# A gated convolution that waits in DRAM as one float32 array and is split into two halves when attention loads it

## The chip, the cores and the metric

The kernel runs on one core of one Trainium2 chip. Its engines are TensorE (PE, with PEld for its weight loads), VectorE (DVE), ScalarE (ACT), GpSimd (POOL) and SyncE (SP), which here issues nearly all transfers between DRAM and the on-chip memory. The metric is the time of one execution on the device in microseconds (us); the number told of a kernel is the median of its runs. The profile is of one further execution, whose own time is given beside its span.

## The reference, cut to what matters

One decoder layer on 1024 tokens of width 1024. A single projection gives ten blocks; four feed a gated convolution, four an attention with 16 heads, two the gates with which the branches are merged.

```python
proj = jnp.einsum("bsd,dc->bsc", h, w_in)
xc, bg, cg, zc, q, k, v, za, g_conv, g_attn = jnp.split(proj, splits, axis=-1)
c = causal_depthwise_conv(cg * xc, conv_w)
y_conv = jnp.einsum("bsc,cd->bsd", jax.nn.silu(zc) * bg * c, w_out_conv)
o = mixture_of_dilations(q, k, v, slopes)
y_attn = jnp.einsum("bsc,cd->bsd", jax.nn.silu(za) * o, w_out_attn)
merged = sigmoid(g_conv) * y_conv + sigmoid(g_attn) * y_attn
return jnp.einsum("bsd,de->bse", merged, w_o)
```

The array of this case is `silu(zc) * bg * c`, here called y: 1024 channels by 1024 tokens, kept in 8 blocks of 128 channels. It is computed early and multiplied by `w_out_conv` much later.

## The kernel before, in words

Every float32 operand of a matmul is written as the sum of a high and a low part in the type float32r. `split(hi, lo, src)` makes them: ScalarE casts (L80), and VectorE, or GpSimd where it is named, subtracts (L81). A product then takes three matmuls (hi x hi, hi x lo, lo x hi).

The program has these stages in time: v (to about 117 us), then the other sections of the projection in pairs (`sec`: q and k, the convolution's four, the gates), attention with its 16 heads (from about 812 us), the attention output, and the last product.

In a section, twelve matmuls make one product, a weight half `a_hi`, `a_lo` is split for it from the tile `raw` or from a sum `s`, and a result leaves the bank through a copy (L352) or an addition `sec_o` (L357). The last section of each channel pair of the convolution ends in `sg` = y (L414). There the kernel before splits `sg` into `qk_hi` (ScalarE) and `qk_lo` (GpSimd) and stores both to `y_dram`, 512 tokens at a time (L415 to L419): 16 pieces. After the convolution the table `tb` for attention's bias is loaded (L426), VectorE computes the bias of the first head (L438), and GpSimd that of each later one (L440, L441).

Attention goes through 64 units, each a head and two query blocks of 128: TensorE makes scores (L462, L463), VectorE adds the bias and finds the extreme `nm` (L467), ScalarE takes exponentials (L472, which also leaves the denominator `den`), TensorE transposes the blocks (L583), ScalarE and VectorE split them into `pp` and `diag` (L80, L81), and TensorE multiplies them by the values `vp` (L594, L595). `scores` runs two units ahead of `values`. Two results of a head are copied out by `otmp` and `ot` (L600, L601). From the second unit of the loop on, every second unit fetches one block c of y into `ghi[:, c]` and `glo[:, c]` (L677 to L680): a tiny copy from `den` into the tile on VectorE comes first, so that the load cannot be issued before attention is that far. Eight blocks of y are fetched in units 2 to 16.

`conv_out(c, h)` is the product of y with `w_out_conv`, 24 matmuls (L98 to L100) for each of 16 pieces; its weights come through `load_w` (L83). The pieces are called from the fifth head on, but their matmuls read one block of y each.

What sets the order: the order of instructions on each engine is not that of the code. The framework sorts them by an estimate of its own of when each could run, and each engine and SP's queue then goes strictly in that order, an instruction that waits holding up all behind it. Tiles named `raw` in the pool `wr` share four buffers of 4 KB per partition, which are given out in the order of the code: first the sections' weights, then in attention the weights and gates (`gc`) of `conv_out`.

Of the kernel before, what the change touches and what calls it, by code (L numbers as in the profile page):

```python
# [11 lines left out]
F32 = mybir.dt.float32  # L12
F32R = mybir.dt.float32r
# [5 lines left out]
P = 128  # L19
S = 1024  # L20
D = 1024
NK = D // P
# [15 lines left out]
def f(ap):  # L38
    return ap.bitcast(F32)
# [3 lines left out]
def layer(ctx, tc, x, norm_g, w_blk, w_v, b_merge, conv_w, w_conv, w_attn, w_o, final_g, tab, sel_in, selb_in, out):  # L43
    nc = tc.nc
# [3 lines left out]
    wr = ctx.enter_context(tc.tile_pool(name="wr", bufs=4, reuse_waits="tile"))  # L48
    small = ctx.enter_context(tc.tile_pool(name="small", bufs=4, reuse_waits="tile"))
    dram = ctx.enter_context(tc.tile_pool(name="dram", bufs=1, space=DRAM))  # L50
# [14 lines left out]
    m_dram = dram.tile([NK, P, S], F32, name="m_dram")  # L65
    r_dram = dram.tile([NP, 32, P], F32, name="r_dram")
    z_dram = dram.tile([NK, P, S], F32, name="z_dram")
    y_dram = dram.tile([2, NK, P, S], F32, name="y_dram")
    g_dram = dram.tile([2, NK, P, S], F32, name="g_dram")
    qk_dram = dram.tile([NP, 4, P, S], F32, name="qk_dram")  # L70

# [7 lines left out]
    def split(hi, lo, src, eng=None):  # L79
        nc.scalar.copy(hi, src)  # L80
        (eng or nc.vector).tensor_sub(lo, src, f(hi))  # L81
# [241 lines left out]
    pc = pc_cm.__enter__()  # L323
# [70 lines left out]
    for c in range(0, NK, 2):  # L394
        xc = pc.tile([P, 2, S], F32, name="xc", bufs=1)
        uu = pc.tile([P, 2, 2 + S], F32, name="uu", bufs=1)
        nc.gpsimd.memset(uu[:, :, 0:2], 0.0)
        for i, t, v in sec(c, c + 1):
            nc.scalar.copy(xc[:, i, t], v)
        for i, t, v in sec(16 + c, 17 + c):  # L400
            nc.vector.tensor_mul(uu[:, i, 2 + t.start:2 + t.stop], v, xc[:, i, t])
        cv = xc
        for i in range(2):
            w3 = cw[:, c + i]
            nc.scalar.mul(cv[:, i], uu[:, i, 2:2 + S], w3[:, 2:3])
            for j in (1, 0):
                nc.vector.scalar_tensor_tensor(cv[:, i], uu[:, i, j:j + S], w3[:, j:j + 1], cv[:, i], op0=OP.mult, op1=OP.add)
        for i, t, v in sec(8 + c, 9 + c):
            nc.vector.tensor_mul(cv[:, i, t], v, cv[:, i, t])
        for i, t, v in sec(24 + c, 25 + c):  # L410
            sg = out_tile()
            nc.scalar.activation(sg, v, AF.Sigmoid)
            nc.vector.tensor_mul(sg, v, sg)
            nc.vector.tensor_mul(sg, sg, cv[:, i, t])  # L414
            hi = pc.tile([P, 512], F32R, name="qk_hi", bufs=1)  # L415
            lo = pc.tile([P, 512], F32R, name="qk_lo", bufs=1)
            split(hi, lo, sg, nc.gpsimd)
            nc.sync.dma_start(y_dram[0, c + i, :, t], f(hi))
            nc.sync.dma_start(y_dram[1, c + i, :, t], f(lo))  # L419
    pc_cm.__exit__(None, None, None)  # L420


# [23 lines left out]
    den, pools = {}, []  # L446
# [95 lines left out]
    with (tc.tile_pool(name="atl", bufs=2, reuse_waits="tile") as atl, tc.tile_pool(name="atm", bufs=2, reuse_waits="tile") as atm,  # L542
# [109 lines left out]
        for i, (hd, bp) in enumerate(units):  # L652
            if i % 4 == 0:
                if hd % 2 == 0:
                    ot[hd // 2] = atl.tile([P, S], F32, name="ot")
                if hd + 1 < NH:
                    load_head(hd + 1)
            if i + LOOK < len(units):
                ready.append(scores(*units[i + LOOK]))
            if i == len(units) - 5:  # L660
                ab = ap0.tile([P, 2, S], F32R, tag="tb", name="a_tb")
                load_act(0, ab[:, 0], ab[:, 1])
                load_act(1, *act_tiles((ap0, "q2", 1), (ap0, "kh", 1)))
                load_act(2, *act_tiles((ap0, "kl", 1), (ap0, "bias", 2)))
            if i == len(units) - 2:
                load_act(3, *act_tiles((ap1, "q2", 1), (ap1, "kh", 1)))
                act7 = act_tiles((ap1, "kl", 1), (ap0, "bias", 2))
                nc.sync.dma_start(f(act7[0]), z_dram[NP - 1])
                sel_b = rrows[1][:32]
                sel_raw = wr.tile([P, S], F32, tag="raw", name="raw")  # L670
                nc.sync.dma_start(sel_raw[:32], selb_in)
                nc.scalar.copy(sel_b, sel_raw[:32])
                gate_last(LAST[1] // 4)
            values(hd, bp, ready.pop(0))
            if i % 2 == 0 and G0 <= i < G0 + 2 * NK:

                c = (i - G0) // 2  # L677
                for g, src in ((ghi, y_dram[0, c]), (glo, y_dram[1, c])):
                    nc.vector.tensor_copy(g[:, c, 0:1], den[hd // 2][:, hd % 2, bp:bp + 1])
                    nc.sync.dma_start(f(g[:, c]), src)  # L680
            if i % 4 == 3:
                if hd in FILLS:
                    conv_out(*divmod(FILLS.index(hd), 2), atn)
                if hd % 2 == 1:
                    divide(hd // 2)
                elif hd:
                    spread(hd // 2 - 1)
                if hd == NH - 1:
                    gate_last(LAST[3] // 4)
                    last_act(*act7)  # L690
                    conv_out(*divmod(FILL, 2), atn)
                    for i in range(FILL + 1, 2 * NK):
                        conv_out(*divmod(i, 2), work, (2, 4))
# [122 lines left out]
```

## Time and profile before

| | |
|---|---|
| median of 3 runs | 1342.55 us (1336.83 to 1343.76) |
| profiled execution | 1339.46 us, its span 1337.7 us |
| TensorE busy | 1290.5 us (96%) |
| VectorE busy | 831.2 us (62%) |
| ScalarE busy | 647.5 us (48%) |
| GpSimd busy | 228.8 us (17%) |
| TensorE's granted clock, mean | 0.988 of full speed |
| moved by DMA | 191.92 MB, of it 58.31 MB written |
| chain of waits that ended last | TensorE 83%, DMA 7%, VectorE 4%, ScalarE 3% |

The shares are means over stages that differ. In the windows view each row is a stretch of time, and for each engine it has the busy time and the number of instructions. "Busy" for a DMA is the mean over the core's 16 DMA engines, and can come out a little above 1. A row of the waits says which instruction stood still, on which engine, and what ended its wait. A row of the timeline has the start, the duration and, in square brackets, the idle time of the engine ahead of it.

### The profile page before, as it was taken

To read this page: it belongs to the slowest core of one execution; us is meant where nothing else is said; L and a number is where in the kernel's file an instruction comes from. 1 tells how busy PE (TensorE), PEld (TensorE's weight loads), DVE (VectorE), ACT (ScalarE), POOL (GpSimd) and SP (SyncE) were. 2 spreads that over 40 slices of the span, in tenths; PEclk is the share of its full clock that TensorE was granted. 3 is DMA by queue.
4 is the path that set the end of the run, shared out by engine and by line. 5 is a ranking of instruction groups with operands and counts; after the bars stand their busy time and mean duration, and the time that the engine had idled before them with its cause. 6 is when DMAs were issued, how large, how long until landed. Compare 5 with 4: busy or idle time off the path is not lost.

```text
span 1337.7 us, 17655 instructions
## 1 busy us (share of the span) xinstructions
PE 1290.5 (96%) x6236; PEld 1069.4 (80%) x6236; DVE 831.2 (62%) x1580; ACT 647.5 (48%) x1271; POOL 228.8 (17%) x170
## 2 busy tenths in 40 slices
PE   9799999999999999999999997889999999999997
PEld 6577888888888888878888886778888988888886
DVE  6965665657677666776554444677677665454325
ACT  7643444444434444344444465777677776222211
POOL 0000000000101000030000002534434455154000
PEclk9999999999999999999999998999999999999999
DMA  7455444422313132163333316986656573555302
GB/s 281 145 173 183 163 173 166 164 81 63 126 48 111 62 102 72 65 211 103 109 120 111 105 63 177 303 228 153 174 145 186 143 241 144 199 189 189 142 32 95
DMA packets 86930, 191.92 MB, mean 143 GB/s; under 512 B 8429, under 2 KB 33261, under 8 KB 86714
## 3 DMA queue, kind: packets, MB, share of 16 engines
q1 hardware_dynamic: 84040, 181.80, 43.1%
q0 software_dynamic: 2800, 9.00, 2.0%
q8 instruction: 49, 0.80, 0.3%
q14 instruction: 39, 0.32, 0.1%
q10 hardware_dynamic: 2, 0.00, 0.0%
HBM read 132.46 MB, written 58.31 MB: 143 GB/s over the span
## 4 chain that ended last, share of the span: by engine, by line
PE 83%; DMA 7%; DVE 4%; ACT 3%; issue 1%; SPq 0%; POOL 0%; DVEq 0%; ACTq 0%
PE bank L346 17%; PE bank L347 17%; PE bank L348 17%; PE bank L98 4%; PE bank L99 4%; PE bank L100 4%; PE bank L583 3%; PE bank L754 2%; PE bank L753 2%; PE bank L752 2%; PE bank L594 2%; PE bank L595 2%; PE bank L462 2%; PE bank L463 2%; DMA v_dram<-v 1%
## 5 line engine op out<-in xcount | busy, mean ns | idle before, releaser
L346 PE MATMUL bank<-t_hi,a_hi 128*128 128x512 f32 x576 | 225.5, 392 | 3.6 <-DVE sec_o L357 3.2
L347 PE MATMUL bank<-t_lo,a_hi 128*128 128x512 f32 x576 | 224.9, 390 | 0.0
L348 PE MATMUL bank<-t_hi,a_lo 128*128 128x512 f32 x576 | 224.9, 390 | 0.0
L80 ACT CAST a_hi<-s 128x512 fp32r<-128x512 f32 x144 | 89.6, 622 | 184.2 <-PE bank L347 167.7
L346 PE MATMUL bank<-b_hi,a_hi 128*128 128x512 f32 x432 | 169.0, 391 | 3.2 <-ACT a_hi L80 3.2
L347 PE MATMUL bank<-b_lo,a_hi 128*128 128x512 f32 x432 | 168.6, 390 | 0.0
L348 PE MATMUL bank<-b_hi,a_lo 128*128 128x512 f32 x432 | 168.4, 390 | 0.0
L81 DVE TENSOR_TENSOR a_lo<-s,a_hi 128x512 fp32r<-128x512 f32 x144 | 103.0, 715 | 93.1 <-ACT a_hi L80 93.1
L80 ACT CAST a_hi<-raw 128x512 fp32r<-128x512 f32 x108 | 67.0, 621 | 145.8 <-PE bank L347 123.3
L346 PEld LDWEIGHTS bank<-t_hi,a_hi 128*128 128x128 f32 x576 | 108.6, 189 | 27.4 <-DVE sec_o L357 3.9
L347 PEld LDWEIGHTS bank<-t_lo,a_hi 128*128 128x128 f32 x576 | 108.7, 189 | 22.5
L348 PEld LDWEIGHTS bank<-t_hi,a_lo 128*128 128x128 f32 x576 | 108.4, 188 | 22.6
L472 ACT ACTIVATE pr<-pr,nm 128x640 f32<-128x640 f32 (+7 forms) x128 | 100.0, 784 | 15.9 <-DVE nm L467 15.4
L346 PEld LDWEIGHTS bank<-b_hi,a_hi 128*128 128x128 f32 x432 | 81.4, 188 | 21.0 <-ACT a_hi L80 4.1
L81 DVE TENSOR_TENSOR a_lo<-raw,a_hi 128x512 fp32r<-128x512 f32 x108 | 74.3, 688 | 36.1 <-ACT a_hi L80 36.1
L348 PEld LDWEIGHTS bank<-b_hi,a_lo 128*128 128x128 f32 x432 | 81.4, 188 | 17.0
L347 PEld LDWEIGHTS bank<-b_lo,a_hi 128*128 128x128 f32 x432 | 81.3, 188 | 16.7
L583 PE MATMUL bank<-ident,pr 128*128 128x128 f32 x576 | 89.7, 276 | 3.3 <-ACT pr L472 2.7
L467 DVE CUSTOM_DVE_ANT_0 pr<-bank,bias 128x512 f32<-128x512 f32 (+3 forms) x128 | 72.0, 569 | 33.6 <-PE bank L463 31.5
L583 PEld LDWEIGHTS bank<-ident,pr 128*128 128x128 f32 x576 | 68.9, 142 | 12.2 <-ACT pr L472 5.3
L81 DVE TENSOR_TENSOR pp<-bank,pp 128x512 fp32r<-128x512 f32 x96 | 64.9, 687 | 19.7 <-ACT pp L80 19.0
L462 PE MATMUL bank<-kh,q 128*128 128x256 f32 (+2 forms) x192 | 73.7, 386 | 1.7 <-ACT sg L492 0.8
(230 smaller groups left out, 2635.3 us busy)
## 6 DMA issues: line engine op xcount, KB each, us to landing
raw<-in_w_blk SPq DMA_DIRECT2D x72, 512.0 KB, 3.6
raw<-in_w_v SPq DMA_DIRECT2D x18, 512.0 KB, 3.8
v_dram<-v SPq DMA_DIRECT2D x16, 512.0 KB, 3.0
qk_dram<-qk_hi SPq DMA_DIRECT2D x32, 256.0 KB, 2.0
qk_dram<-qk_lo SPq DMA_DIRECT2D x32, 256.0 KB, 2.8
q<-qk_dram SPq DMA_DIRECT2D x32, 256.0 KB, 8.1
kh<-qk_dram SPq DMA_DIRECT2D x32, 256.0 KB, 6.4
kl<-qk_dram SPq DMA_DIRECT2D x32, 256.0 KB, 7.5
```

Source lines behind the costliest of these rows:

```text
L80: nc.scalar.copy(hi, src)
L81: (eng or nc.vector).tensor_sub(lo, src, f(hi))
L98: nc.tensor.matmul(pt, whi[:, k, :], mhi[:, t], start=(k == 0), stop=False)
L99: nc.tensor.matmul(pt, whi[:, k, :], mlo[:, t], start=False, stop=False)
L100: nc.tensor.matmul(pt, wlo[:, k, :], mhi[:, t], start=False, stop=(k == NK - 1))
L346: nc.tensor.matmul(pt, hi[:, k], mhi[:, k], start=first and k == 0, stop=False, **more)
L347: nc.tensor.matmul(pt, hi[:, k], mlo[:, k], start=False, stop=False, **more)
L348: nc.tensor.matmul(pt, lo[:, k], mhi[:, k], start=False, stop=k == H - 1, **more)
L462: nc.tensor.matmul(sc[:, :n], qs, kh[hd][:, c0:c0 + n], start=True, stop=False)
L467: nc.vector.tensor_tensor_reduce(pr[:, c0:c0 + m], sc[:, :m], bias[hd][:, off:off + m], 1.0, 3.0e38 if nm is None else nm, OP.add, OP.min, ...
L472: nc.scalar.activation(pr[:, :nk], pr[:, :nk], AF.Exp, bias=nm, scale=-1.0, accum_out=den[p][:, a, b:b + 1])
L583: nc.tensor.transpose(pt[:, j, i * P:(i + 1) * P], rows[b][:, (kb + j) * P:(kb + j + 1) * P], ident)
```

## The change

y goes through DRAM once, in float32. The split before the store is gone, `sg` itself is stored; a block that comes back lands in a tile `raw`, and `split` makes `ghi[:, c]` and `glo[:, c]` of it, on ScalarE and VectorE. The tiny copy from `den` now goes to `raw`.

```diff
-    y_dram = dram.tile([2, NK, P, S], F32, name="y_dram")
+    y_dram = dram.tile([NK, P, S], F32, name="y_dram")
...
             nc.vector.tensor_mul(sg, sg, cv[:, i, t])
-            hi = pc.tile([P, 512], F32R, name="qk_hi", bufs=1)
-            lo = pc.tile([P, 512], F32R, name="qk_lo", bufs=1)
-            split(hi, lo, sg, nc.gpsimd)
-            nc.sync.dma_start(y_dram[0, c + i, :, t], f(hi))
-            nc.sync.dma_start(y_dram[1, c + i, :, t], f(lo))
+            nc.sync.dma_start(y_dram[c + i, :, t], sg)
...
                 c = (i - G0) // 2
-                for g, src in ((ghi, y_dram[0, c]), (glo, y_dram[1, c])):
-                    nc.vector.tensor_copy(g[:, c, 0:1], den[hd // 2][:, hd % 2, bp:bp + 1])
-                    nc.sync.dma_start(f(g[:, c]), src)
+                raw = wr.tile([P, S], F32, tag="raw", name="raw")
+                nc.vector.tensor_copy(raw[:, 0:1], den[hd // 2][:, hd % 2, bp:bp + 1])
+                nc.sync.dma_start(raw, y_dram[c])
+                split(ghi[:, c], glo[:, c], raw)
```

Lines behind the first edit stand four lower in the changed kernel, and behind the second three lower (L472 becomes L468, L438 becomes L434).

On ScalarE, in the third head, the rows of the kernel before, from the exponential of its sixth block to that of its eighth (`rt` belongs to the denominators):

```order
L472 ACTIVATE pr_7208,den<-pr_7208,nm 128x768
L615 CAST rt<-bank 32x128
L80 CAST diag_6700<-bank 128x256
L80 CAST diag_6701<-bank 128x128
L472 ACTIVATE pr_7237,den<-pr_7237,nm 128x896
L80 CAST diag_6700<-bank 128x128
L80 CAST pp<-bank 128x512 x2
L600 COPY otmp<-bank 64x512
L601 COPY ot<-bank 64x512
L472 ACTIVATE pr_7249,den<-pr_7249,nm 128x1024
```

On ScalarE the changed kernel has at that place:

```order
L468 ACTIVATE pr_7119,den<-pr_7119,nm 128x640
L80 CAST ghi<-raw 128x1024
L468 ACTIVATE pr_7131,den<-pr_7131,nm 128x768
L80 CAST diag_6621<-bank 128x256
L80 CAST diag_6620<-bank 128x256
L80 CAST pp<-bank 128x512 x2
L468 ACTIVATE pr_7161,den<-pr_7161,nm 128x896
L80 CAST diag_6621<-bank 128x128
L80 CAST ghi<-raw 128x1024
L80 CAST diag_6620<-bank 128x128
L468 ACTIVATE pr_7173,den<-pr_7173,nm 128x1024
```

The fourth and fifth block of y are cast here, between exponentials; before, nothing on ScalarE read y.

On VectorE, where the first bias is computed behind the convolution, the kernel before:

```order
L336 TENSOR_TENSOR s_4976<-raw 128x512
L81 TENSOR_TENSOR a_lo<-raw,a_hi 128x512
L357 TENSOR_TENSOR sec_o<-bank,u_4904 128x512
L81 TENSOR_TENSOR a_lo<-raw,a_hi 128x512
L438 SCALAR_TENSOR_TENSOR bias<-tb 128x1024
L483 TENSOR_TENSOR sg<-sec_o,sg 128x512
```

On VectorE the changed kernel has there:

```order
L336 TENSOR_TENSOR s_4896<-raw 128x512
L434 SCALAR_TENSOR_TENSOR bias<-tb 128x1024
L81 TENSOR_TENSOR a_lo<-raw,a_hi 128x512
L357 TENSOR_TENSOR sec_o<-bank,u_4824 128x512
L81 TENSOR_TENSOR a_lo<-raw,a_hi 128x512
L479 TENSOR_TENSOR sg<-sec_o,sg 128x512
```

The bias, which reads `tb`, has moved ahead of two `a_lo` and one `sec_o`.

On SP, at the second block of y, the kernel before (`kl` is a key half, `vp` the values):

```order
L435 DMA kl<-qk_dram 64x1024 x2
L680 DMA ghi<-y_dram 128x1024
L680 DMA glo<-y_dram 128x1024
L87 DMA raw<-in_w_conv 128x1024
L512 DMA raw<-g_dram 128x1024
L87 DMA raw<-in_w_conv 128x1024
L564 DMA vp<-v_dram 128x8x128
```

On SP the changed kernel has there the following:

```order
L431 DMA kl<-qk_dram 64x1024 x2
L676 DMA raw<-y_dram 128x1024
L560 DMA vp<-v_dram 128x8x128
L676 DMA raw<-y_dram 128x1024
L431 DMA kh<-qk_dram 64x1024
```

The second half of y and the early weights have left this place of the queue; in the changed kernel the first `in_w_conv` stands right behind the eighth load of y.

## Rows read from the trace of the kernel before

**Rows 1.** Windows of 10 us: PE, PEld, DVE, ACT, POOL busy (instructions), clock, DMA share, GB/s.
```profile
300.00:310.00 10.00, 10.00 (x46) 8.29 (x45) 7.54 (x11) 3.62 (x7) 0.00 (x0) 1.00 0.26 76
590.00:600.00 10.00, 7.13 (x25) 5.46 (x25) 6.96 (x6) 2.24 (x4) 6.17 (x2) 0.84 1.03 285
```

**Rows 2.** The same view, windows of 20 us where the convolution comes back.
```profile
820.00:840.00 20.00, 19.16 (x115) 16.93 (x116) 14.06 (x48) 13.52 (x33) 7.46 (x4) 0.86 1.05 244
840.00:860.00 20.00, 15.95 (x96) 13.43 (x95) 10.58 (x38) 14.20 (x34) 11.48 (x6) 0.91 1.04 313
860.00:880.00 20.00, 15.06 (x97) 12.61 (x96) 14.84 (x48) 15.30 (x37) 10.21 (x5) 1.00 1.06 285
880.00:900.00 20.00, 19.84 (x135) 18.15 (x134) 13.46 (x42) 14.48 (x39) 5.25 (x4) 0.91 0.74 222
```

**Rows 3.** Waits of PE, 795 to 930: us in total, times, longest us.
```profile
PE bank L98 <- DMA ghi<-y_dram: 4.9, 2, 3.5
PE bank L98 <- ACT w_hi L80: 3.0, 1, 3.0
PE bank L594 <- ACT ot L601: 1.5, 1, 1.5
PE bank L99 <- DMA glo<-y_dram: 0.8, 1, 0.8
```

**Rows 4.** Waits of ACT, 795 to 930.
```profile
ACT otmp L600 <- DMA m_dram<-sg: 4.9, 1, 4.9
ACT w_hi L80 <- DMA raw<-in_w_conv: 4.0, 1, 4.0
```

**Rows 5.** Tiles, lines, timeline: ns min/median/max or busy us, mean ns; start us, us.
```profile
L418 SPq DMA_DIRECT2D y_dram<-qk_hi x16: 319/320/327, 336.3 to 581.9; - x16
...
L81 POOL TENSOR_TENSOR qk_lo<-sg,qk_hi x16: 1289/1574/1823, 336.4 to 581.9; 128x512 fp32r<-128x512 f32 x16
...
L81 DVE TENSOR_TENSOR w_lo<-raw,w_hi x8: 1215/1226/2733, 1147.5 to 1220.1; 128x1024 fp32r<-128x1024 f32 x8
...
L80 ACT CAST w_hi<-raw 128x1024 fp32r<-128x1024 f32 x16 | 16.9, 1053 | 24.6 <-PE bank L99 20.6 <-DMA raw<-in_w_conv 4.0
...
572.58 1.58 POOL L81 TENSOR_TENSOR qk_lo<-sg,qk_hi 128x512 fp32r<-128x512 f32 x1 [6.41 <-ACT qk_hi L80]
573.17 1.53 DVE L413 TENSOR_TENSOR sg<-sec_o,sg 128x512 f32<-128x512 f32 x1 [0.17 <-ACT sg L412]
```

**Rows 6.** Timeline where tb is loaded: start us, us, instruction, [idle before <-releaser].
```profile
585.89 0.68 DVE L81 TENSOR_TENSOR a_lo<-raw,a_hi 128x512 fp32r<-128x512 f32 x1
592.94 1.23 DVE L438 SCALAR_TENSOR_TENSOR bias<-tb 128x1024 f32<-128x1024 f32 x1 [4.04 <-DMA tb<-in_tab]
...
585.58 0.33 SPq L426 DMA_DIRECT2D tb<-in_tab  x1
...
596.26 0.50 PE L346 MATMUL bank<-t_hi,a_hi 128*128 128x512 f32 x1 [2.87 <-DVE sec_o L357]
```

**Rows 7.** Timeline of SP: issues of ghi, second, fourth, sixth.
```profile
830.71 0.53 SPq L680 DMA_DIRECT2D ghi<-y_dram  x1
...
852.58 0.33 SPq L680 DMA_DIRECT2D ghi<-y_dram  x1
...
869.74 0.35 SPq L680 DMA_DIRECT2D ghi<-y_dram  x1
```

**Rows 8.** Timeline of ACT: exponentials of these heads.
```profile
833.68 0.73 ACT L472 ACTIVATE pr<-pr,nm 128x512 f32<-128x512 f32 x1
...
854.58 0.84 ACT L472 ACTIVATE pr<-pr,nm 128x640 f32<-128x640 f32 x1
...
870.65 0.83 ACT L472 ACTIVATE pr<-pr,nm 128x640 f32<-128x640 f32 x1 [0.17 <-DVE nm L467]
```

**Rows 9.** Landing us of ghi; DMA issues 900 to 935: count, KB each, median us.
```profile
DMA to landing us min/median/max: 9.3/9.8/10.6
...
vp<-v_dram SPq DMA_DIRECT2D x3, 512.0 KB, 5.0
```

## The prediction

> **What bounds the kernel now.** I read the profile in this order: the windows table, the waits of the matrix engine and of ScalarE in the stretch where the convolution comes back, then single instructions there. The windows table says where a saving can reach the end at all. While the gated convolution is computed and stored (300 to 590 us) TensorE is busy 10.00 of 10 us in each of the 29 windows of 10 us; the first stands in [rows 1], and the one after them is the first with a hole (7.13 of 10, clock 0.84). ScalarE and VectorE have time to spare in that stretch. The second place is the first heads of attention: from 820 to 880 us the DMA engines show a share of 1.04 to 1.06, TensorE is busy 15.95 and 15.06 of 20 us in two windows, and the granted clock is 0.86 and 0.91 of full speed [rows 2], where full speed is the 2.4 GHz level and a dip is time at 1.2 GHz. The waits name the cause [rows 3]: TensorE stands 4.9 us for ghi from y_dram, 0.8 us for glo and 3.0 us for a weight cast w_hi, 8.7 us in all. That cast waits itself: ScalarE stood 4.0 us for the weight's transfer [rows 4]. So in the early heads the conv matmuls, mixed one by one into attention, are stopped by transfers that share a full DMA system with q, k, v.
>
> **The change, part by part.**
>
> *Before the store.* 16 casts qk_hi on ScalarE and 16 subtractions qk_lo on GpSimd (1.574 us each, 25.2 us [rows 5]) go. TensorE hides them all (10.00 of 10 busy), so they pay 0; were TensorE not in front, the 25.2 us would be the most they could give. The new store reads sg, of which there are two buffers; I cost that at 0 by the same cover.
>
> *Where the table tb is loaded.* In the order, VectorE's bias (L438 before, L434 after) moves ahead of two a_lo and a sec_o; SP issues tb before a z store and not behind it. Before, tb was issued at 585.58, bias began at 592.94 after a wait of 4.04, and TensorE stood 2.87 us until 596.26 [rows 6]; with the clock of 0.84 in that window (0.16 x 10 = 1.6 us) the place cost 4.5 us. After, tb can go once the last y store is issued, which the last hi store dates to 581.9 [rows 5]: 3.7 us earlier. With the same 7.4 us to arrive it is there at about 589.5. But bias now stands in front of work that ran at 585.89 [rows 6], so the wait of VectorE is nearly as long, and behind it queue a_lo, sec_o, a_lo (0.68 each): the second a_lo ends at 589.5 + 1.23 + 3 x 0.68 = 592.8, and the matmul that it feeds is due between 590 and 593. That is a stop of 0 to 2.8 us in place of 2.87. Bounds: -4.5 (no stop at all) and +3 (a second stop of the old size). I take -1.0, since the wait stays.
>
> *The waits that go.* glo is no longer loaded: 8 transfers of 512 KB fewer in the stretch. The w_hi casts of the first weights now stand behind the eighth y load, since all of these share the four raw buffers in order. The matmuls on ghi and glo move to the fifth head. So TensorE's 8.7 us are taken away: -8.7. The clock dips that followed the two longest stops (0.91 in two windows of 20 us: 1.8 us each [rows 2]) go with them, -3.6, if nothing new stops TensorE.
>
> *The split that comes.* Eight casts of 128x1024 at 1.053 us on ScalarE [rows 5] are 8.4 us. From 820 to 880 ScalarE is busy 43.0 of 60 us and VectorE 39.5 [rows 2]; with the conv matmuls gone from these heads and the stalls taken out, ScalarE is the engine that paces them, so the casts have little cover. Price between 0 (all of it swallowed in waits that exist anyway) and 8.4; the nearest row is the 4.0 us stall of ScalarE that reached TensorE as 3.0 [rows 3, 4], a ratio of 0.74: +6.2. The eight subtractions glo are 8 x 1.226 = 9.8 us on VectorE [rows 5], beside ScalarE on the slightly less busy engine: 0 on the path, up to 9.8 if that cover is gone; the 16 one-column casts that become 8 are nothing.
>
> *The waits that come.* This decides it. A cast ghi stands in ScalarE's queue, and exponentials and the casts pp and diag stand behind it; VectorE and then TensorE wait for those. Where it stands is fixed by the order. For the second, fourth and sixth block I set the time at which its load was issued [rows 7] against the end of the exponential behind which the cast now stands [rows 8]. Second: 833.68 + 0.73 - 830.71 = 3.7 us. Fourth: 854.58 + 0.84 - 852.58 = 2.8.  Sixth: 870.65 + 0.83 - 869.74 = 1.7. That is 8.2 us in three places; the other five blocks have more time, or their load is already under way while ScalarE waits for the one before. How long it takes to land: 9.8 us at a share above 1 in this stretch, and 5.0 us for vp (also 512 KB) after it [rows 9]. Seven glo of 0.52 MB, 3.7 of the (244 + 313 + 285) x 20 us = 16.8 MB moved from 820 to 880 [rows 2], and the first weights leave the stretch, so I take 6.0, near the lower row. ScalarE then waits 3 x 6.0 - 8.2 = 9.8 us (6.8 at 5.0; 21.2 at 9.8). Two stalls of ScalarE are seen to reach TensorE: 4.0 as 3.0, and 4.9 (otmp for a store) as 1.5 [rows 3, 4], so 0.74 and 0.31, mean 0.52: +5.1. Bounds: 6.8 x 0.31 = 2.1 and 21.2 x 0.74 = 15.7. For the clock I take smaller dips, but more of them, in place of two: 0 net, bounds -3.6 and +3.6.
>
> *Sum.* -1.0 - 8.7 + 6.2 + 5.1 + 0 = +1.6 us. On the profiled execution (1339.46: span 1337.7 and 1.8 around it) that is 1341.1; that execution lies 3.1 under the median of the runs, 1342.55, on which the same difference gives 1344.2. I forecast 1344, near the second, as the time asked for is a median.
>
> **A rule against the change.** w_lo, a subtraction on VectorE of just the shape of the new glo, took 1.226 us at the median and 2.733 at the most [rows 5]. The Trainium skill, GPSIMD Engine Reference, Key points, says that GpSimd shares its SBUF interfaces with VectorE and collides with VectorE instructions that have two SBUF inputs; the trace fits, as L413 took 1.53 us while GpSimd worked on qk_lo [rows 5]. In attention the new glo is such an instruction (pp, diag and the score reduction read PSUM for one input). By that rule the eight subtractions are slow wherever they meet the bias work of GpSimd; what it would make of the time is the third rival.
>
> **Rivals.**
>
> *Faster: the full DMA system was the price, and the rest hides.* For it: of TensorE's 9.0 us without work from 840 to 880 [rows 2] 8.7 are these waits, and half the bytes of y leave. Then -8.7 - 3.6 for the stops and dips, -4.5 for the tb place, the casts at half price (+4.2) and the waits at their low bound (+2.1): -10.5, time 1332. Against it: the three places leave a load at most 3.7 us.
>
> *Slower: ScalarE stopped at the head of its queue.* One mechanism: loads that are issued behind a batch of q, k loads land as late as before (9.8 us), and ScalarE, unlike TensorE before, holds up everything. Waits +15.7 in place of 5.1, casts in full 8.4, dips +3.6: 1.6 + 10.6 + 2.2 + 3.6 = +18.0, time 1360.5. It decides from a landing of about 8 us on (3 x 8 - 8.2 = 15.8 us of waiting, 11.7 at 0.74). For it: the second and fourth loads are issued right behind such a batch. Against it: less is in flight.
>
> *Slower: VectorE becomes the bound.* All eight glo at 2.733: 21.9 us and not 9.8. VectorE from 820 to 880 then has 39.5 + 21.9 = 61.4 against ScalarE's 43.0 + 8.4 = 51.4: 10 us over; 1.6 + 10 on the median is 1354. Against it: at the median of 1.226 it has 49.3 and stays below.
>
> **How the numbers follow.** The forecast has a chance of 0.43 (its own range 1337 to 1351, by the bounds of casts and tb), the faster case 0.26, the first slower one 0.20, the second 0.08, and 0.03 is left for none of them. About 0.5% (6.7 us) is what a measurement of this kernel can tell from no change: 1335.8 to 1349.3. Of the forecast's chance 0.32 lies in that band, 0.02 below and 0.09 above; of the faster case 0.22 below; of the slower ones 0.24 above. With the small rest shared out that makes 0.25 faster, 0.41 within, 0.34 slower. The range that leaves 2 in 10 out is 1333 to 1359.
>
> **What would show it.** Right: in the profile after, TensorE's waits for ghi and glo from y_dram are gone, ScalarE shows waits of ghi for y_dram of 7 to 15 us in three to five places, the DMA share from 820 to 880 is below 0.9, and 300 to 580 is as full as before. The forecast is wrong if ScalarE hardly waits for y_dram (under 4 us: then faster), if y lands in more than 8 us (then slower), or if the glo subtractions take over 2 us on the mean. The tb step is wrong if TensorE's stop near 593 is longer than 2.9 us.

## The result

The changed kernel takes 1349.62 us (median of 8 runs, 1343.32 to 1355.14) against 1342.07 us (8 runs, 1336.83 to 1343.76): a ratio of 1.0068, 95% interval 1.0041 to 1.0095. That is 7.6 us slower by the medians and 9 by the ratio, small, but clear of no change. The forecast was 1344; the time lies inside its range (1333 to 1359) and inside the forecast's own (1337 to 1351). Its size was not foreseen: the sum had +1.6 us, and the likeliest outcome (0.41) was a time that can't be told from no change.

The profiled execution of the changed kernel took 1355.01 us (span 1353.1), one of its slower ones; of the other runs four lie at 1347.3 to 1349.7, so some 5 us of what this profile shows does not stand in the median. That matters below. The bytes moved fell from 191.92 to 183.52 MB.

The windows of the changed kernel, with the columns of [rows 1, 2]:

```profile
300.00:580.00 280.00, 280.00 (x1237) 231.88 (x1236) 191.62 (x282) 112.15 (x184) 0.31 (x3) 1.00 0.22 71
590.00:600.00 10.00, 9.55 (x42) 7.59 (x42) 8.95 (x11) 3.88 (x7) 4.12 (x2) 1.00 0.87 259
820.00:840.00 20.00, 16.86 (x93) 14.84 (x91) 14.62 (x36) 13.33 (x31) 6.42 (x3) 0.82 0.80 188
840.00:860.00 20.00, 17.51 (x107) 13.67 (x107) 16.95 (x52) 16.95 (x40) 8.41 (x4) 1.00 0.70 178
860.00:880.00 20.00, 14.53 (x83) 12.14 (x83) 15.77 (x43) 16.05 (x37) 7.74 (x4) 0.91 0.63 166
880.00:900.00 20.00, 16.51 (x104) 13.40 (x104) 15.38 (x44) 14.67 (x36) 9.14 (x5) 0.98 0.87 263
1090.00:1100.00 10.00, 8.39 (x60) 7.29 (x59) 5.59 (x19) 7.30 (x18) 4.37 (x3) 1.00 0.61 176
1130.00:1140.00 10.00, 7.77 (x47) 6.55 (x46) 4.87 (x10) 5.60 (x13) 6.94 (x6) 0.90 0.32 116
1140.00:1150.00 10.00, 10.00 (x34) 8.19 (x33) 3.62 (x6) 2.40 (x4) 2.30 (x3) 0.59 0.44 144
```

Read them in three parts. The convolution is as full as before (280 of 280), and the hole at 590 is nearly closed (9.55 of 10 at full clock, 7.13 at 0.84 before). From 820 to 880 the DMA share is down to 0.63 to 0.80, but TensorE is no fuller than in [rows 2]: 48.9 of 60 us busy, 50.2 before. And there is a part that the prediction does not speak of: holes at 1090 and 1130, the second with the clock at 0.59 behind it. In the kernel before TensorE is nearly full there, at full clock (the same columns):

```profile
1090.00:1110.00 20.00, 19.48 (x115) 15.95 (x114) 12.66 (x40) 16.24 (x38) 14.37 (x13) 1.00 0.58 198
1130.00:1150.00 20.00, 20.00 (x92) 16.64 (x91) 7.87 (x11) 3.46 (x5) 5.89 (x6) 1.00 0.63 224
```

TensorE's and ScalarE's waits from 795 to 930, as in [rows 3, 4]:

```profile
PE bank L590 <- ACT ot L597: 5.3, 2, 3.7
PE bank L579 <- ACT pr L468: 3.9, 2, 2.1
PE bank L458 <- DVE nm L463: 2.5, 9, 0.4
PE bank L590 <- ACT pp L80: 2.3, 1, 2.3
PE bank L98 <- ACT w_hi L80: 0.6, 1, 0.6
...
ACT ghi L80 <- DMA raw<-y_dram: 10.8, 7, 2.8
```

TensorE no longer waits for y at all. It waits for what ScalarE and VectorE make (ot, pr and pp, nm), 14.0 us in these four rows against 4.3 for the same tiles before, and ScalarE waits 10.8 us for y.

To compare many kernels I use one worked-out number per stretch, TensorE's lost time: in windows of 5 us, the width minus busy time times granted clock, added up. It holds idle time and time at the lower clock alike. It is not exact (before to after it explains some 10 of the 15.4 us between the two spans, as a busy time can hide small gaps), and a fixed window does not hold the same work in every kernel (the wait of 3.2 us for vp ends at 820.4 in the kernel before, that of 3.1 us at 817.7 in the changed one), but it says where to look.

| lost us | 580-620 | 820-900 | 900-960 | 960-1050 | 1050-1160 |
|---|---|---|---|---|---|
| before | 4.2 | 15.8 | 2.8 | 0.6 | 1.2 |
| changed | 0.5 | 19.9 | 1.6 | 1.0 | 11.2 |
| e1_store_side | 0.6 | 18.0 | 4.2 | 0.6 | 2.2 |
| e2_load_side | 3.8 | 20.6 | 3.2 | 1.0 | 9.6 |
| e3_cast_later | 0.6 | 12.2 | 2.9 | 0.8 | 1.8 |
| e7 (e3 once more) | 0.6 | 11.1 | 2.2 | 0.8 | 1.6 |
| e4_own_buffers | 0.5 | 14.9 | 2.3 | 0.6 | 2.0 |
| e5_cast_by_token | 0.8 | 17.3 | 0.9 | 0.3 | 3.3 |
| e6_own_buffers_later | 0.9 | 13.8 | 1.1 | 0.6 | 2.7 |
| e8_casts_doubled | 0.6 | 10.0 | 5.1 | 0.9 | 1.8 |
| e9_late_heads | 0.6 | 22.4 | 0.9 | 0.8 | 1.1 |
| e10_control | 2.1 | 20.8 | 1.9 | 1.0 | 4.3 |
| e11_cast_two_units | 0.9 | 14.3 | 7.7 | 8.0 | 1.6 |
| e12_subs_doubled | 0.7 | 14.9 | 4.7 | 0.3 | 0.9 |

The row "changed" against "before": a gain at tb, a loss in the early heads, and in this execution the largest difference in the last heads, hundreds of us behind the edit. A mark of equal work helps: when the 110th exponential starts, TensorE has 5020 to 5023 matmuls behind it in each of these kernels, 216 of the 384 conv matmuls among them. It starts at 1073.1 us in the kernel before and at 1079.1 in the changed one, so 6.0 of the 15.4 us between the spans are lost ahead of it and 9.4 behind.

### The profile page after: what moved, and what is told of

It is laid out like the page before. It is cut to its first block, busy times and chain, and to the rows that moved or that the text cites. A ratio compares the mean times of both kernels' runs of the same rounds, so it can differ in the third digit from the quotient of the medians.

```text
span 1353.1 us, 17592 instructions
## 1 busy us (share of the span) xinstructions
PE 1301.5 (96%) x6236; PEld 1078.0 (80%) x6236; DVE 831.7 (61%) x1580; ACT 647.4 (48%) x1263; POOL 205.1 (15%) x154
## 2 busy tenths in 40 slices
DMA packets 83473, 183.52 MB, mean 136 GB/s; under 512 B 8045, under 2 KB 32877, under 8 KB 83258
## 5 line engine op out<-in xcount | busy, mean ns | idle before, releaser
L81 DVE TENSOR_TENSOR a_lo<-s,a_hi 128x512 fp32r<-128x512 f32 x144 | 99.2, 689 | 99.8 <-ACT a_hi L80 99.7
L468 ACT ACTIVATE pr<-pr,nm 128x640 f32<-128x640 f32 (+7 forms) x128 | 99.8, 781 | 9.5 <-DVE nm L463 9.1
L579 PE MATMUL bank<-ident,pr 128*128 128x128 f32 x576 | 93.1, 283 | 7.1 <-ACT pr L468 5.5
L346 PEld LDWEIGHTS bank<-b_hi,a_hi 128*128 128x128 f32 x432 | 81.4, 188 | 20.6 <-ACT a_hi L80 3.8
```

Source lines behind the costliest of these rows:

```text
L346: nc.tensor.matmul(pt, hi[:, k], mhi[:, k], start=first and k == 0, stop=False, **more)
L468: nc.scalar.activation(pr[:, :nk], pr[:, :nk], AF.Exp, bias=nm, scale=-1.0, accum_out=den[p][:, a, b:b + 1])
L579: nc.tensor.transpose(pt[:, j, i * P:(i + 1) * P], rows[b][:, (kb + j) * P:(kb + j + 1) * P], ident)
```

## The experiments

Ratios are to the kernel before, run on the same chip in the same job. e1 to e4, e5 to e8 and e9 to e12 ran in three jobs on three chips, so kernels of different jobs are compared by their ratios. The names A, B, C and D are those of the expectations.

**One side of the change at a time.** e1 stores as the changed kernel does and loads both halves from the one array; e2 stores as before and loads as the changed kernel does.

```diff
 e1, against the changed kernel:
-     nc.sync.dma_start(raw, y_dram[c])
-     split(ghi[:, c], glo[:, c], raw)
+     for g, src in ((ghi, y_dram[c]), (glo, y_dram[c])):
...
+         nc.sync.dma_start(f(g[:, c]), src)
 e2, against the kernel before:
-     for g, src in ((ghi, y_dram[0, c]), (glo, y_dram[1, c])):
...
+     nc.sync.dma_start(raw, y_dram[0, c])
+     split(ghi[:, c], glo[:, c], raw)
```

> Only the store side of the change: the gated convolution is stored once in float32 without a split, and both halves of attention's copy are loaded from that one array (so the values of the low half are not the reference's). On every engine attention's order is that of the kernel before. Theory 1 (the store side gains at the place of tb, the load side costs more): TensorE's stop near 593 us shrinks from 2.87 us to under 1, the clock of that window stays at full speed, and the time is about 4 us below the kernel before (1338 against 1342, ratio 0.997). Theory 2 (the store side is worth nothing, as TensorE covers it): ratio 1.000. Theory 3 (the store side is what costs, as the two buffers sg are now held until the store has landed): ratio above 1.004.

> Only the load side: y is split and stored in two halves as before, and attention loads one array (the high half) into raw and splits it there (so the low half's values are not the reference's). Attention's order is that of the changed kernel. Theory 1: the load side costs some 12 us, time about 1354 (ratio 1.009), with TensorE's stop near 593 us as in the kernel before (2.9 us). Theory 3 (the store side costs): ratio 1.000.

e1: ratio 1.000 (0.9984 to 1.0016). e2: 1.0074 (1.0047 to 1.0102), median 1353.10. So the load side bears the whole loss. Theory 1 was right on the place and wrong on the time of e1: the stop near 595 us did shrink from 2.87 to 0.61 us, and attention's fifth exponential, the first behind the sections, started 3.0 us earlier (812.48, 815.51 before); but the gain was given back in the early heads (18.0 + 4.2 lost against 15.8 + 2.8; this execution, of 1345.49 us, is the slowest of e1's twelve, so a part of that is its own), where both halves still had to come:

```profile
PE bank L98 <- ACT w_hi L80: 3.7, 1, 3.7
PE bank L99 <- DMA glo<-y_dram: 2.8, 3, 1.2
PE bank L98 <- DMA glo<-y_dram: 2.6, 1, 2.6
PE bank L98 <- DMA ghi<-y_dram: 2.3, 3, 1.4
```

These waits of TensorE in e1 (same stretch as [rows 3]) sum to 11.4 us, 8.7 before. A stage that starts earlier in front of its transfers would wait for them longer; that this is what happened was not tested. e2 says the same of the gain: on every engine its order in attention is that of the changed kernel, its fifth exponential starts 3.6 us later (816.58, 813.00), and the ratios differ by 0.06%.

**ScalarE's wait, and the gaps that conv matmuls filled.** In e3 a one-column copy from a later denominator goes into `ghi[:, c]` ahead of the split, which so comes later; the load stays. e4 gives the blocks of y two buffers of their own.

```diff
 e3:
+ ywait = {}
...
      nc.sync.dma_start(raw, y_dram[c])
-     split(ghi[:, c], glo[:, c], raw)
+     ywait[i + 3] = c, raw
+ if i in ywait:
+     c, raw = ywait.pop(i)
+     nc.vector.tensor_copy(ghi[:, c, 0:1], den[hd // 2][:, hd % 2, bp:bp + 1])
+     split(ghi[:, c], glo[:, c], raw)
 e4:
-     raw = wr.tile([P, S], F32, tag="raw", name="raw")
+     raw = work.tile([P, S], F32, tag="yraw", name="yraw", bufs=2)
```

> The changed kernel, with each cast ghi held back by a one-column copy from a later denominator, so that it stands 3 to 5 exponentials later on ScalarE; the loads and the conv matmuls stay where they were. Theory A (ScalarE stopped at the head of its queue is the price): ScalarE's wait for y_dram falls from 10.8 us to under 3, and the time by about 5 us against the changed kernel, to 1344 to 1345 (ratio 1.002). Theory B (the price is that no conv matmul fills TensorE's gaps in heads 2 to 4 any more): the waits fall likewise, but the time stays within 2 us of the changed kernel, 1348 to 1351 (ratio 1.006), and TensorE's idle time from 820 to 900 us (14.6 us in the changed kernel) stays above 12.

> The changed kernel, with two buffers of their own for the blocks of y that come back, so that the first weights of conv_out no longer stand behind the eight y loads in the four buffers raw: the order has 9, 15, 21 and 24 conv matmuls done by the end of the second to fifth head, as in the kernel before, in place of 0, 0, 0 and 24. The casts ghi stand where they stood, give or take 2 exponentials. Theory B: TensorE's idle time from 820 to 900 us falls by 8 us or more, and the time to about 1340 (ratio 0.998). Theory A: ScalarE still waits some 10 us for y_dram, and the time stays within 3 us of the changed kernel (ratio 1.004 to 1.008).

e3: ratio 0.9963 (0.9946 to 0.998), median 1337.77, faster than both kernels. e4: 1.0016 (0.9999 to 1.0033), median 1345.63, between the two theories; ScalarE still waited 9.8 us. In e3 ScalarE has no wait for y_dram left; its early windows:

```profile
820.00:840.00 20.00, 18.79 (x121) 16.18 (x121) 15.50 (x50) 16.52 (x39) 7.74 (x4) 0.94 1.01 235
840.00:860.00 20.00, 17.89 (x121) 15.08 (x120) 18.91 (x58) 19.22 (x49) 10.53 (x6) 1.00 0.76 192
860.00:880.00 20.00, 15.77 (x106) 13.12 (x104) 18.88 (x51) 17.86 (x45) 10.12 (x5) 1.00 0.87 218
880.00:900.00 20.00, 18.09 (x103) 15.44 (x103) 12.84 (x39) 12.81 (x26) 6.97 (x4) 0.91 0.76 212
```

ScalarE is busy 53.6 of 60 us from 820 to 880, 46.3 in the changed kernel: the waits have become work. But the gain (12 us by the medians, 14 by the ratios) is over twice the 5 of theory A, and e3 loses 1.8 us in the last heads where the changed kernel loses 11.2. The edit had changed the order there too. So the next runs were to part these.

**Is it the order of the last heads?** e5 uses the same copies from a denominator two units earlier than e3 (its expectation says one).

```diff
 e5:
+     ywait[i + 1] = c, raw      # i + 3 in e3_cast_later
```

> The changed kernel with the same one-column copies as in e3_cast_later, but from a denominator one unit earlier: the casts ghi stand where they stood in the changed kernel (behind the same exponential for six blocks, two later for two), so they should still stop ScalarE, while the order of the last heads comes out as in the kernel before (the weight of the 14th head's conv piece cast behind exponential 98, the casts of a_tb behind 117, and 20 conv matmuls one transpose group earlier). Theory A (ScalarE's wait for y is nearly the whole price): ScalarE waits 8 us or more for y_dram and the time stays at 1347 to 1351 (ratio 1.004 to 1.007). Theory C (half of the price is the other order of the last heads, where the changed kernel's TensorE had holes and a clock dip from 1130 to 1146 us): the waits stay, but the time falls to 1341 to 1344 (ratio 1.000), with TensorE full at 1.00 clock from the last head on.

e5: 1.0015 (1.0002 to 1.0027), median 1344.80, which comes near theory C. But both theories wanted the waits to stay, and they had not: 4.6 us in three places. A cleaner pair followed, e9 and e10, which differ from the changed kernel by two one-column copies on ScalarE deep in attention.

```diff
+ if i == 42:                    # e9; 40 in e10
+     for _ in range(2):
+         nc.scalar.copy(den[hd // 2][:, hd % 2, bp:bp + 1], den[hd // 2][:, hd % 2, bp:bp + 1])
  if i == len(units) - 5:
```

> The changed kernel with two one-column copies on ScalarE (den onto itself) in unit 42, the 11th head. Up to the 84th exponential every engine's order is exactly that of the changed kernel; from there on the order of the last heads comes out as in the kernel before (the weight cast behind exponential 98 and not 99, the first cast of a_tb behind 117 and not 116, 21 conv matmuls three groups of transposes earlier). Theory C (most of the loss is the order of the last heads, which the change has shifted as a by-product): the time falls to 1341 to 1344 (ratio 0.999 to 1.002), with ScalarE's early waits for y_dram still at 9 to 12 us. Theory A (the early waits are the price): 1347 to 1351 (ratio 1.004 to 1.007).

> The control of e9_late_heads: the same two copies two units earlier, where they change nothing else of the order of any engine. Theories A and C alike: as the changed kernel, 1348 to 1352 (ratio 1.005 to 1.008), with TensorE's stop and clock dip at the end of the last head. If it comes out as e9_late_heads, the copies themselves and not the order make the difference.

e9: 1.0017 (0.9999 to 1.0035), median 1345.88. e10: 1.0069 (1.0045 to 1.0094), median 1350.08, just the changed kernel's ratio. e10's order is that of the changed kernel throughout, but for the two copies. e9's is the same until the 84th exponential, and so are the times: that one starts at 1013.08 in the changed kernel, 1013.57 in e9, 1013.33 in e10. ScalarE's early waits are 10.6 and 11.3 us. From there on e9's order differs, and behind the 100th exponential it is that of the kernel before. e9 and e10 differ by 0.52% by the ratios (7.0 us; 4.2 by the medians). Most of it falls behind the mark of equal work, the 110th exponential, which starts in e9 and in e10 at:

```profile
1078.67 0.94 ACT L468 ACTIVATE pr<-pr,nm 128x768 f32<-128x768 f32 x1
...
1079.66 0.96 ACT L468 ACTIVATE pr<-pr,nm 128x768 f32<-128x768 f32 x1
```

That is 1.0 us apart; the spans (1342.8 and 1347.5) are 4.7 apart. Against the kernel before, e9 is 5.6 us late at the mark and 5.1 at the end (that kernel's profiled execution lies 2.6 us under its median, e9's 1.0), so what e9 still loses is lost ahead of the last heads. The order decides there what ScalarE meets first. Around its exponential 117 (128x640) ScalarE has in the changed kernel:

```
L80 CAST diag_6620<-bank 128x256
L80 CAST a_tb<-act 128x512
L468 ACTIVATE pr_10225,den<-pr_10225,nm 128x640
L596 COPY otmp<-bank 64x512
```

In e9, as in the kernel before, it has this exponential ahead of the cast `a_tb`:

```
L80 CAST diag_6621<-bank 128x256
L468 ACTIVATE pr_10227,den<-pr_10227,nm 128x640
L80 CAST diag_6620<-bank 128x256
L80 CAST diag_6621<-bank 128x128
L80 CAST a_tb<-act 128x512
```

`a_tb` is an operand of the attention output, needed only later, and made from a product on GpSimd that is not ready (GpSimd stood 6.25 us for a load of it). Two rows of ScalarE's timeline and three of TensorE's in the changed kernel (start, us, what; idle before):

```profile
1096.94 0.62 ACT L80 CAST a_tb<-act 128x512 fp32r<-128x512 f32 x1 [1.84 <-POOL act L530]
1097.47 0.82 ACT L468 ACTIVATE pr<-pr,nm 128x640 f32<-128x640 f32 x1
...
1098.44 0.33 PE L579 MATMUL bank<-ident,pr 128*128 128x128 f32 x1 [1.22 <-ACT pr L468]
1099.64 0.39 PE L590 MATMUL bank<-diag,vp 128*128 128x256 f32 x1 [0.40 <-ACT ot L597]
1138.16 0.58 PE L590 MATMUL bank<-diag,vp 128*128 128x256 f32 x1 [1.16 <-ACT ot L597]
```

ScalarE waits 1.84 us for GpSimd in front of an exponential, TensorE then stops 1.22 us for that exponential. At 1138 the last head ends without a conv matmul in its gaps: in this order the conv piece there stands in one block ahead of the last transposes, and none between these and the last products with vp (three come ahead of the very last one). In e9 and in the kernel before, five conv matmuls and the eight matmuls that spread the last denominators (L631) stand among them. (The expectation misread this: in e9 two groups of 20 and 21 conv matmuls stand one group of transposes earlier, and three conv matmuls later.) Windows of the last heads in e10:

```profile
1090.00:1100.00 10.00, 8.66 (x61) 7.47 (x59) 6.07 (x18) 7.18 (x17) 4.08 (x3) 1.00 0.65 191
1130.00:1140.00 10.00, 8.20 (x57) 6.82 (x56) 5.39 (x11) 5.54 (x13) 5.91 (x5) 1.00 0.41 142
1140.00:1150.00 10.00, 10.00 (x46) 8.26 (x45) 4.39 (x7) 2.40 (x4) 2.32 (x3) 1.00 0.60 225
```

The same windows in e9:

```profile
1090.00:1100.00 10.00, 10.00 (x75) 9.11 (x74) 8.36 (x27) 9.27 (x24) 8.19 (x6) 1.00 0.57 194
1130.00:1140.00 10.00, 9.84 (x62) 8.46 (x61) 4.95 (x10) 4.72 (x11) 4.75 (x4) 1.00 0.46 157
1140.00:1150.00 10.00, 10.00 (x46) 8.28 (x45) 3.87 (x6) 1.54 (x3) 2.68 (x4) 1.00 0.69 238
```

In e10 the holes are those of the changed kernel, without the clock at 0.59 behind them; its profiled execution took 1349.37, the changed kernel's 1355.01. The 5.3 us that the two differ in lost time from 1110 to 1160 (7.5 and 2.2) are about the 5.6 between these two executions. e2, which has the changed kernel's order there, shows the same stop of 1.16 us, and the dip (clock 0.56 from 1140 to 1150). So the stop at the end of the last head is followed by the dip in two profiled executions of three; that the dip is what parts the changed kernel's execution from e10's is argued, not shown.

**Do the early waits cost anything then?** e11 is e3 with the copies one unit earlier; in the last heads it has the order of the kernel before. e6 has both remedies of e3 and e4 (split two units late, own buffers).

```diff
 e11:
+     ywait[i + 2] = c, raw      # i + 3 in e3_cast_later
```

> e3_cast_later with the copies from one unit earlier: casts ghi behind exponentials 10, 13, 18, 21, 28, 30, 36, 38, and the last heads in the order of the kernel before (e3_cast_later has an order of its own there). Theory A+C (late heads and early waits add up; without the waits some 4 to 6 us more than e9_late_heads are won): 1336 to 1340 (ratio 0.995 to 0.998). Theory C alone (e3_cast_later won by its order in the last heads, the early waits cost next to nothing): 1341 to 1344 (ratio 1.000).

> Both remedies: two buffers of their own for y and casts held back by one more unit, so that they stand 1 to 7 exponentials later than with the buffers alone. Conv matmuls are again mixed into the second to fifth head (6, 15, 21 and 24 done). Theory A: ScalarE's waits for y_dram fall from 9.8 us to under 4, the time to 1335 to 1339 (ratio 0.996). Theory B (the filled gaps are worth something of their own): it comes out below e3_cast_later, at 1331 to 1335 (ratio 0.993). A rival to both: TensorE now waits for ghi and glo itself, as in the kernel before, and the time is 1342 (ratio 1.000).

e11: 1.0103 (1.0068 to 1.0138), median 1356.42, the slowest of all and expected by no theory. The early stretch is what theory A + C wanted: ScalarE waits 0.3 us for y, and TensorE loses 14.3 us from 820 to 900 in place of 19.9. But 15.7 are lost from 900 to 1050, 2.6 in the changed kernel. Two waits of TensorE and ScalarE in e11 from 900 to 1050:

```profile
PE bank L590 <- ACT ot L597: 6.6, 6, 1.6
...
ACT otmp L596 <- DMA m_dram<-sg: 18.1, 4, 5.6
```

ScalarE stands four times for a store of a conv piece (otmp and that piece's sg share one buffer), 18.1 us. That is the same kind of accident as in the last heads, in the middle ones: e11's 110th exponential starts at 1089.4. e6: 0.9984 (0.9972 to 0.9996), median 1340.44: ScalarE's wait 2.2 us, 13.8 lost in the early stretch. Theory B's further gain did not come; TensorE instead stood 4.7 us for w_hi. ScalarE's waits for y in e4 and in e6:

```profile
ACT ghi L80 <- DMA yraw<-y_dram: 9.8, 5, 2.5
...
ACT ghi L80 <- DMA yraw<-y_dram: 2.2, 2, 1.7
```

In all five kernels without most of the wait (e3, e6, e8, e11, e12) TensorE loses 10.0 to 14.9 us from 820 to 900, in the four that keep it on the buffers raw (changed, e2, e9, e10) 19.9 to 22.4; e4, which keeps the wait but has conv matmuls in the gaps, 14.9. e5, with 4.6 us of the wait left, loses 17.3. In the kernels whose gaps are empty the wait so goes with 5 us or more of lost time there.

How much of that reaches the end, three comparisons tell. First, e4 and e6 are parted by one edit, the place of the casts, and behind the 53rd exponential every engine has the order of the kernel before in both. With 9.8 us of waits e4 is at 1.0016 (0.9999 to 1.0033), with 2.2 us e6 at 0.9984 (0.9972 to 0.9996): 0.32%, 4.3 us. Second, e9 and e3, without conv matmuls in the gaps, differ by 0.54% (7.2 us). Their orders are not the same behind, but their times there are: e3's 110th exponential starts at

```profile
1072.49 0.96 ACT L468 ACTIVATE pr<-pr,nm 128x768 f32<-128x768 f32 x1
```

(1071.1 in e7), 6.2 us ahead of e9's, and from it to the end e3 takes 263.5 us, e9 264.1. So theory A holds beside theory C: the changed kernel's late heads cost 4 to 7 us and its early waits about as much. Third, e4 and e9 have like waits (9.8 and 10.6 us) and one order behind the 100th exponential; e4 has conv matmuls in the gaps of the early heads and e9 has none, and their ratios are 1.0016 and 1.0017. The filled gaps, theory B, are worth nothing that can be seen at the end (the intervals leave some 3 us either way).

**The price of the split's work.** e8 casts each ghi twice, e12 subtracts each glo twice, both on e3. The run labelled e7_two_casts is e3 again, with nothing cast twice, as a measure of how one kernel's profile repeats.

```diff
 e8:
+     nc.scalar.copy(ghi[:, c], raw)
      split(ghi[:, c], glo[:, c], raw)
 e12:
      split(ghi[:, c], glo[:, c], raw)
+     nc.vector.tensor_sub(glo[:, c], raw, f(ghi[:, c]))
```

> A second look at e3_cast_later (nothing changed) for its profile: TensorE's idle time from 820 to 900 us within 1.5 us of the 9.5 us read there; time 1335 to 1341.

> e3_cast_later with each cast ghi done twice, so 8 casts of 1.05 us (8.4 us) more on ScalarE at places where it does not wait for the load. Theory A (a stopped ScalarE is the price, work on it is not, or little): within 3 us of e3_cast_later, 1336 to 1341 (ratio 0.996 to 0.999). Theory D (any time of ScalarE in these heads, work or wait, reaches the end in full): 8 us above, about 1346 (ratio 1.003).

> e3_cast_later with each subtraction glo done twice: 8 x 1.23 = 9.8 us more on VectorE. The order of the last heads is that of the kernel before. If work on VectorE is hidden in these heads, as the prediction put it: within 3 us of e11_cast_two_units. If VectorE counts like ScalarE: 5 us or more above it, 1342 or more (ratio 1.001).

e7: 1336.34 in its one run; TensorE idle 7.9 us from 820 to 900 against 9.5, 0.1 outside what was expected. e8: 1.0001 (0.9984 to 1.0019), median 1342.28: 0.38% or 5.1 us above e3 for 8.4 us of casts, between A and D; a share of 0.6. Behind the 53rd exponential its order is e3's on every engine, so this is the price of the casts and not of an order behind them. e12: 1.0027 (1.001 to 1.0044), median 1345.66. Its yardstick e11 had failed; against e3 it is 0.64% (8.6 us) for 9.8 us of subtractions, in another order of the heads behind. In its profile VectorE has become the full engine of one early window:

```profile
860.00:880.00 20.00, 16.11 (x100) 13.51 (x98) 20.00 (x48) 13.41 (x35) 7.69 (x5) 0.91 0.65 179
```

VectorE is busy 20.00 of 20 us, ScalarE 13.41; one of the subtractions took 4.57 us there, beside two operations of GpSimd. So the doubled subtractions seem not to be hidden, but the order behind them is another; that the single ones are was not shown either.

## Why the prediction was right or wrong, step by step

**The convolution's stage: nothing, as priced.** TensorE 280 of 280, with 16 casts and 16 subtractions gone; e1 as a whole is at 1.000.

**The place of tb: right direction, at the edge of its bounds.** -1.0 was taken with -4.5 as the bound; the lost time fell by 3.7 (4.2 to 0.5). The rows answer to [rows 6]:

```profile
587.85 1.23 DVE L434 SCALAR_TENSOR_TENSOR bias<-tb 128x1024 f32<-128x1024 f32 x1 [2.28 <-DMA tb<-in_tab]
589.00 1.52 DVE L81 TENSOR_TENSOR a_lo<-raw,a_hi 128x512 fp32r<-128x512 f32 x1
590.44 0.68 DVE L357 TENSOR_TENSOR sec_o<-bank,u 128x512 f32<-128x512 f32 x1
591.04 0.68 DVE L81 TENSOR_TENSOR a_lo<-raw,a_hi 128x512 fp32r<-128x512 f32 x1
```

tb was issued at 582.06, as early as reckoned, and arrived in 5.8 us, not 7.4, so bias began 1.6 us sooner than the 589.5 of the sum, and the a_lo behind it were in time. e1 shows, though, that what is gained here was not seen at the end.

**"So TensorE's 8.7 us are taken away": the step that failed in the early heads.** The waits for y and w_hi went (8.7 to 0.6 us), and TensorE lost 19.9 us there in place of 15.8. Without conv matmuls to mix in, the heads 2 to 5 run at ScalarE's pace, and TensorE waits 14.0 us for ot, pr, pp and nm, 4.3 before: 9.7 us more of such waits for 8.1 less of the old ones. The sum has for this stretch -8.7 + 6.2 + 5.1 = +2.6 us; in the profiled executions the lost time rose by 4.1, and by 7.3 with the wait for vp that only the kernel before has inside the window. A wait that ends last is not saved in full when another engine is right behind it. How much of the 8.7 was saved at the end no run shows by itself.

**The casts: near.** 8 casts at 1.048 us; priced at 0.74 of their time, measured on doubled ones 0.6.

**ScalarE's waits: right in sum and price, wrong in place.** Taken were 9.8 us, priced at 5.1, at the second, fourth and sixth block, from a landing of 6.0 us. The loads landed in 6.4 us at the median (3.1 to 6.6), and the waits were 10.8 us, in seven places. At the end such waits are worth 4.3 us (e4 against e6) to 7.2 (e9 against e3). Three of the eight casts:

```profile
828.60 1.04 ACT L80 CAST ghi<-raw 128x1024 fp32r<-128x1024 f32 x1 [2.54 <-DMA raw<-y_dram]
872.06 1.04 ACT L80 CAST ghi<-raw 128x1024 fp32r<-128x1024 f32 x1 [2.50 <-DMA raw<-y_dram]
894.84 1.04 ACT L80 CAST ghi<-raw 128x1024 fp32r<-128x1024 f32 x1 [2.85 <-DMA raw<-y_dram]
```

The sixth, at 872.06, was foretold; the first and the eighth, said to "have more time", waited as long, while the second and the fourth waited 0.62 and 0.97. The slack was taken from the times of the kernel before; with ScalarE and the queue both moved, it is a guess for a single place.

**What the sum left out: the heads behind.** It has no term after the fifth head. The changed kernel loses 11.2 us from 1050 to 1160, 1.2 before, and e9 against e10 shows 4 to 7 us of the time behind the 84th exponential, with the order ahead of it unmoved. This is the term that the sum lacks, and the largest part of what it missed. The prediction showed the order at the edit's places and did not look at the last heads, where the new order could have been seen (a_tb ahead of the 640-column exponential). With the old order in the last heads restored (e9), the change measures 1.0017, +2.3 us (-0.1 to +4.7 by the interval; 4.1 by the medians): beside the +1.6 of the sum. That agreement is partly luck: the gain at tb did not reach the end and the old stops were not saved in full, while the casts were priced 1.1 us too high, and e9's own number is known to some 2 us only. That the measured time fell into the stated range is due to the range's width, as the late heads stood in no term and in no rival.

**The rivals.** Faster (the DMA system was the price): the DMA share did fall to 0.63 to 0.80, and TensorE was not fuller for it. Slower by ScalarE's queue: it decides from a landing of 8 us, and 6.4 was measured; its mechanism is that of the forecast, its size did not come. Slower by VectorE: three of the eight glo were slow, all while GpSimd worked on the next bias, and five met no work of GpSimd and took 1.23. Three of the eight, and GpSimd's bias at the first:

```profile
829.67 2.91 DVE L81 TENSOR_TENSOR glo<-raw,ghi 128x1024 fp32r<-128x1024 f32 x1 [1.40 <-ACT ghi L80]
838.19 1.23 DVE L81 TENSOR_TENSOR glo<-raw,ghi 128x1024 fp32r<-128x1024 f32 x1
849.00 2.13 DVE L81 TENSOR_TENSOR glo<-raw,ghi 128x1024 fp32r<-128x1024 f32 x1 [1.32 <-ACT ghi L80]
...
829.14 2.35 POOL L437 TENSOR_TENSOR bias<-bias,tb 128x1024 f32<-128x1024 f32 x1
```

The mean of the eight is 1.64 us, under the 2 that was named as the mark. The Trainium skill, GPSIMD Engine Reference, Key points, says that GpSimd shares its interfaces to SBUF with VectorE and collides with VectorE instructions with two SBUF inputs; the trace agrees (1.23 alone, 1.95 to 2.91 beside GpSimd). It is not so each time: in e3 one of these subtractions took 1.22 us beside the first step of a bias (857.13 to 859.91). In the changed kernel it is a tax on three instructions, not a bound.

## What to carry to other kernels

Where a scheduler writes the order, an edit's price has two parts: its own, and that of every place behind it where the order falls out differently; compare the orders of the whole program, and look where a cast for a later stage now stands ahead of the work of this one. Measure such a change beside a control that shifts the order and nothing else: here two one-column copies moved the time by 0.5%, three quarters of what the change itself did (0.7%). And an instruction that reads a fresh load should stand, on an in-order engine, some units behind the load (0.32% between e4 and e6, with one order behind; e3 beat both kernels so, at 0.9963). But an order that falls out badly can take more than that back: e11, with the waits gone, was the slowest of all.

## What was not expected of the hardware

A stop of 1.16 us at the end of the last head is followed, in two profiled executions (the changed kernel and e2), by a granted clock of 0.59 and 0.56 from 1140 to 1150 us, and in a third with the same stop (e10) by full clock. At 0.59 most of that stretch ran at the 1.2 GHz level. The three differ in what TensorE did some 3 us ahead of the stop: there it also stood 0.73 us in the changed kernel and 0.79 in e2, but 0.31 in e10. Whether that decides was not tested.
